# A decoder block on one Trainium2 core: rows of an expert table fetched without pacing, gate weights spread by one float32 matmul a token, and all 72 expert blocks ahead multiplied in whole float32

## The chip, the cores and the metric

One core of a Trainium2 chip runs one program. The metric is the device time of one execution in microseconds (us). Before the change the median of three runs is 1886.55 us (1883.9 to 1891.71). All rows below come from one profiled execution of 1878.31 us, whose span from the first to the last instruction is 1876.5 us.

## The reference, cut to what matters

512 tokens of width 1024 pass two token mixers and then an expert mixer (PEER) of 16384 experts; each token uses 128 of them (8 heads, 16 each). `u` and `v` have one row of 1024 for each expert.

```python
h = rms_norm(x, norm1_g)
proj = h @ w_in                                   # 1024 x 6400
y_a = hgrn2_mixer(...); y_b = dilated_attention_mixer(...)
merged = sigmoid(ga) * (y_a @ w_branch_a) + sigmoid(gb) * (y_b @ w_branch_b)
x = x + merged @ w_out
x = x + peer_ffn(rms_norm(x, norm2_g), w_q, sub_keys, u, v)

def peer_ffn(x, w_q, sub_keys, u, v):
    ...                                           # top 16 of two key sets, then top 16 of their sums: idx, gate
    hid = einsum('thkd,td->thk', u[idx], x)
    a = gelu(hid) * gate
    return einsum('thk,thkd->td', a, v[idx])
```

## The kernel before, in words

The 512 tokens are four tiles of 128 (0 to 3). They go through these stages, with their times in the profiled execution:

- **Front of tile 0** (to about 190 us): projections, both mixers, output projection, query projection.
- **Front of tiles 1 to 3** (190 to 705 us): the same for three tiles at once (`Front`, with `split`: each weight block `w` is loaded from HBM by SP (512 KB, two buffers), ScalarE rounds it to `wh`, VectorE or GpSimd forms the rest `wl` (`halves`, L98 and L99), and TensorE multiplies three products of halves (`accumulate`, L112)). First `mixers`: the projections of the HGRN2 mixer, its chunks, those of the attention, the attention, the gates. Then `post`: the branch products (L479), the output projection (`W_OUT`, added to x at L494), the norm (L500, L512), transposes, the query projection (`W_Q`).
- Beside it tile 0 is routed (`routing`: its experts and gates) and the **rows of u** of tile 0 are worked through: 128 steps, in each of which GpSimd issues an indirect DMA (`row`, L648) that fetches for each of the 128 tokens one row of u (128 x 1024 float32, 512 KB) and VectorE multiplies it with the token's vector and sums (L660). A row's buffer is one of three `rq` and one `row`, used in turn. `background`, called at each load of a weight block, asks for 1.8 such steps (`ROWS_F`) and sets `behind` to that load: by a manual dependency the row's DMA then waits until the weight load has landed. What is left of the 128 steps stands in `post` just ahead of the norm (`before_h2`).
- **The blocks ahead** (705 to 1065 us): `hidden(b)` for the first 72 (`NPRE`) of 128 blocks of experts: a block of `u` (tile `ub`, 512 KB) is multiplied with the 256 tokens of tiles 1 and 2, and GELU is taken. Blocks whose number divides by 3 (24 of 72) go as halves in three float32r products (tiles `uh`, `ul`), the others whole in float32 (tile `h32`, shown as `h`). Between them stand `routing` of tiles 3, 1 and 2, rows of u of tile 3, and the **scatter** (`scatter_steps`).
- **The scatter** writes for the tiles 1, 2 and 0 a dense table of weights, 128 x 128 experts for each token. It goes by groups of 4 tokens (96 groups in all; 4 groups to a `Gx` tile, which then goes to `g_d` in HBM). VectorE compares the two halves of the expert numbers with a ramp (`e12`, L697, bfloat16), multiplies the second with the three bfloat16 parts of the weight (`eg`, L701; in 88 groups the third part is done by ScalarE, four instructions, L705), TensorE does three bfloat16 matmuls a token (L711), ScalarE copies the sum out of PSUM (L713). Whatever of it is left after block 71 is drained (`scat(P)`), 1065 to 1126 us here.
- **The dense v stage** (1126 to 1845 us): 128 blocks of v, with the other 56 blocks of u as halves among them; rows of u and v of tile 3 beside it.

The order on each engine is made by a scheduler that works in the order of the program with a model of its own; each engine then runs its queue strictly in that order.

Of the kernel before, what the change touches and what calls it, by code (L numbers as in the profile page):

```python
# [18 lines left out]
P = 128  # L19
# [29 lines left out]

ROWS_F = 1.8  # L50

NPRE, RING = 72, 56

SPLIT = 3

ROUTE1, ROUTE2, SCAT_H = 12, 30, 2

GS, EGB = 4, 2
ACT3 = {0: (0, 4, 8, 12), 1: (0, 4, 8, 12), 2: (0, 4, 8)}

# [13 lines left out]
def kernel(ctx: ExitStack, tc: tile.TileContext, x, wst, par, cst, cols, g2, keys, u, v, ut, vr, out):  # L74
# [72 lines left out]
    class Front:  # L147
# [320 lines left out]

        def post(self, before_h2=lambda: None):

# [35 lines left out]
            h2s = hp.tile([P, NM // P, D], F32, name="pairA")  # L506
            before_h2()
            for t, T in enumerate(self.tiles):
# [36 lines left out]
    def route_bank(T):  # L545
        bank[0] += 1
        pt = pvg.tile([P, 512], F32, name="vg") if T and bank[0] % 2 else pr.tile([P, 512], F32, name="pr")
        return pt.rearrange("p (n k) -> p n k", k=NKEY)

    def thirds(i, x):  # L550

        w, dst = pk3[:, i], pk[:, i, 2:]
        nc.vector.tensor_copy(dst[:, 0], x)
        nc.vector.tensor_tensor(out=w, in0=x, in1=dst[:, 0], op=ALU.subtract)
        nc.vector.tensor_copy(dst[:, 1], w)
        nc.vector.tensor_tensor(out=w, in0=w, in1=dst[:, 1], op=ALU.subtract)
        nc.vector.tensor_copy(dst[:, 2], w)

    def routing(T, rq):
# [66 lines left out]
        if T in VD:  # L626
            pt = route_bank(T)
            i12 = rt.tile([P, 4, NKEY], F32, name="ssb")

            nc.vector.tensor_scalar(i12[:, 0], full, 1.0 / NKEY, -63.5 / NKEY, op0=ALU.mult, op1=ALU.add)  # L630
            nc.vector.tensor_scalar(i12[:, 0], i12[:, 0], RND, RND, op0=ALU.add, op1=ALU.subtract)
            nc.vector.scalar_tensor_tensor(i12[:, 1], i12[:, 0], -float(NKEY), full, op0=ALU.mult, op1=ALU.add)
            for j in range(2):
                nc.tensor.transpose(pt[:, 1 + j], i12[:, j], ident)
            nc.vector.tensor_copy(pk[:, VD.index(T), 0:2], pt[:, 1:3])
            if T in UD:
                nc.tensor.transpose(pt[:, 3], gate, ident)
                thirds(VD.index(T), pt[:, 3])

# [16 lines left out]
    def u_steps(T):  # L656
        g = UG.index(T)
        for j in range(P):
            r = row(idx[:, g, j:j + 1], u)
            nc.vector.scalar_tensor_tensor(r, r, 1.0, h2g[T], op0=ALU.mult, op1=ALU.mult,  # L660
                                           accum_out=hid[:, g, j:j + 1])
            yield 1
        with tc.high_priority():
            nc.scalar.activation(hid[:, g], hid[:, g], AF.Gelu)
            nc.vector.tensor_mul(hid[:, g], hid[:, g], gates[:, T])
            if T in VD:
                pt = pvg.tile([P, 512], F32, name="vg")
                nc.tensor.transpose(pt[:, :P], hid[:, g], ident)
                thirds(VD.index(T), pt[:, :P])

# [19 lines left out]
    def scatter_steps(T, bank):  # L690
        for i in range(0, P, GT):
            gi = VD.index(T) * (P // GT) + i // GT
            Gx = gb.tile([P, NKEY, GT], F32, name="Gx", bufs=2)
            for k in range(0, GT, GS):
                e = pk[:, VD.index(T), :, None, i + k:i + k + GS]
                e12 = gb.tile([P, 2, NKEY, GS], BF16, name="e12", bufs=2)
                nc.vector.tensor_tensor(out=e12, in0=iota[:, None].to_broadcast([P, 2, NKEY, GS]),  # L697
                                        in1=e[:, 0:2].to_broadcast([P, 2, NKEY, GS]), op=ALU.is_equal)
                eg = gb.tile([P, 3, NKEY, GS], BF16, name="eg", bufs=EGB)
                n = 2 if k in ACT3[T] else 3  # L700
                nc.vector.tensor_tensor(out=eg[:, :n], in0=e12[:, 1:2].to_broadcast([P, n, NKEY, GS]),  # L701
                                        in1=e[:, 2:2 + n].to_broadcast([P, n, NKEY, GS]), op=ALU.mult)
                if n == 2:
                    for q in range(GS):
                        nc.scalar.activation(eg[:, 2, :, q], e12[:, 1, :, q], AF.Copy,  # L705
                                             scale=pk3[:, VD.index(T), i + k + q:i + k + q + 1])
                for q0 in range(0, GS, 4):
                    pt = bank().rearrange("p (n k) -> p n k", k=NKEY)
                    for q in range(4):
                        for j in range(3):  # L710
                            nc.tensor.matmul(pt[:, q], e12[:, 0, :, q0 + q], eg[:, j, :, q0 + q],  # L711
                                             start=(j == 0), stop=(j == 2))
                    nc.scalar.activation(Gx[:, :, k + q0:k + q0 + 4].rearrange("p i t -> p t i"), pt, AF.Copy)  # L713
# [62 lines left out]

    pk = gat.tile([P, len(VD), 5, P], BF16, name="pk", bufs=1)
    pk3 = gat.tile([P, len(VD), P], F32, name="pk3", bufs=1)
    rctx = ctx.enter_context(ExitStack())
# [4 lines left out]
    def background(load):  # L784
        behind[:] = [load]
        rows(min(ROWS_F, P - rows.done))

# [3 lines left out]
    mixers(f)  # L791
    rq1, rq2, rq3 = f.post(lambda: rows(2 * P))
    hH, hL = f.hu
# [11 lines left out]
    def hidden(b, pool):  # L805
# [10 lines left out]
        pt = pool.tile([P, NU], F32, name="ph")  # L816
        if b < NPRE and b % SPLIT:
            accumulate(pt, [ub[:, k] for k in range(KC)], h32, slice(None), True)
# [123 lines left out]
```

## Time and profile before

| | |
|---|---|
| median of 3 runs | 1886.55 us |
| the profiled execution, and its span | 1878.31 us, 1876.5 us |
| TensorE busy | 1684.9 us, 90% of the span |
| VectorE busy | 1373.0 us, 73% |
| ScalarE busy | 784.2 us, 42% |
| GpSimd busy | 637.7 us, 34% |
| mean granted TensorE clock | 0.937 of 2.4 GHz |

Busy time of a matmul includes the drain of its pipeline, so that successive matmuls overlap; how long one really holds the engine is read from the starts of successive ones. One float32 matmul is two records in the trace, one of float32r or bfloat16 is one. "Idle before" in brackets behind a row is the time its engine had nothing running ahead of it, with what ended it.

### The profile page before, as it was taken

What the parts mean: (1) busy time and instruction counts of PE and PEld (TensorE: products, weight loads), DVE (VectorE), ACT (ScalarE), POOL (GpSimd) and SP (SyncE); (2) the same over time, 40 slices, a digit from 0 to 9 for tenths busy, and PEclk for the clock granted to TensorE, in tenths of its full rate; (3) what the DMA queues carried; (4) which work ended last, traced back from release to release, by engine and by line L of the source; (5) the groups of instructions that cost most, each with busy time, mean ns of one, the idle gap of its engine ahead of it and who ended that gap; (6) DMA issues with size and microseconds to landing.
All of it is one profiled execution on the core that took longest, in us unless ns stands there. A gap on an engine that the chain in (4) does not pass through costs nothing.

```text
span 1876.5 us, 28078 instructions
## 1 busy us (share of the span) xinstructions
PE 1684.9 (90%) x10301; PEld 1496.5 (80%) x10301; DVE 1373.0 (73%) x2793; ACT 784.2 (42%) x1466; POOL 637.7 (34%) x502
## 2 busy tenths in 40 slices
PE   8998889788986599999999889999999999989995
PEld 7887888687775489988899778888888888877774
DVE  2114999956567748988899777787778877777874
ACT  3324443333342436662366793343334333323331
POOL 0000455732323301434444104433434334444431
PEclk9999989889997789999999869999999999999998
DMA  8776478766567724755666539999999988888885
GB/s 277 249 234 206 137 249 292 226 230 197 174 213 241 280 79 146 276 208 201 213 223 208 208 127 346 325 343 325 337 321 337 343 314 309 311 287 309 311 301 179
DMA packets 173386, 473.49 MB, mean 252 GB/s; under 512 B 14784, under 2 KB 62144, under 8 KB 173248
## 3 DMA queue, kind: packets, MB, share of 16 engines
q1 hardware_dynamic: 115840, 268.47, 41.9%
q0 software_dynamic: 55296, 201.35, 30.5%
q10 hardware_dynamic: 2112, 1.88, 0.3%
q8 instruction: 81, 1.33, 0.3%
q14 instruction: 57, 0.47, 0.1%
HBM read 442.80 MB, written 27.79 MB: 251 GB/s over the span
## 4 chain that ended last, share of the span: by engine, by line
PE 51%; DMA 24%; DVE 14%; issue 5%; ACT 3%; POOL 2%; DVEq 0%; ACTq 0%; POOLq 0%; SPq 0%
PE acc L873 19%; PE ph L112 15%; PE pp L112 10%; DMA Gc<-g_d 7%; DMA w<-in_wst_dram 6%; PE pg L711 5%; DMA rq<-in_u_dram,idx 4%; DMA row<-in_u_dram,idx 2%; DVE rq L660 2%; DVE wl L99 2%; DMA rowx<-in_u_dram,idx 2%; DMA rowx<-in_v_dram,idx 1%; DVE Gc L862 1%; ACT eg L705 1%; DVE row L660 1%
## 5 line engine op out<-in xcount | busy, mean ns | idle before, releaser
L873 PE MATMUL acc<-vl,ah 128*128 128x512 f32 x768 | 242.3, 395 | 8.2 <-DVE vl L869 8.1
L873 PE MATMUL acc<-vh,al 128*128 128x512 f32 x768 | 241.4, 392 | 0.0
L873 PE MATMUL acc<-vh,ah 128*128 128x512 f32 x768 | 224.7, 398 | 10.8 <-ACT vh L867 10.8
L648 POOL DMA_INDIRECT rowx<-in_u_dram,idx x96 | 125.0, 1302 | 221.0 <-ACT pre L822 61.6
L648 POOL DMA_INDIRECT rowx<-in_v_dram,idx x96 | 133.0, 1385 | 189.2 <-DVE h2g L679 90.8
L112 PE MATMUL ph<-hH,ul 128*128 128x256 f32 x640 | 183.5, 287 | 8.2 <-DVE ul L99 8.2
L112 PE MATMUL ph<-hH,uh 128*128 128x256 f32 x640 | 187.2, 293 | 3.6 <-ACT pre L822 3.6
L112 PE MATMUL ph<-hL,uh 128*128 128x256 f32 x640 | 183.1, 286 | 0.0
L112 PE MATMUL ph<-h,ub 128*128 128x256 f32 x768 | 178.3, 387 | 4.2 <-DMA ub<-in_ut_dram 4.1
L660 DVE SCALAR_TENSOR_TENSOR rq<-rq,h2g 128x1024 f32<-128x1024 f32 x96 | 128.1, 1338 | 66.6 <-DMA rq<-in_u_dram,idx 66.5
L873 PEld LDWEIGHTS acc<-vl,ah 128*128 128x128 f32 x768 | 144.3, 190 | 40.2 <-DVE vl L869 11.7
L98 ACT ACTIVATE ah<-Gc 128x384 fp32r<-128x384 f32 x128 | 67.0, 524 | 261.1 <-PE acc L873 255.9
L873 PEld LDWEIGHTS acc<-vh,ah 128*128 128x128 f32 x768 | 144.3, 191 | 39.6 <-ACT vh L867 12.2
L648 POOL DMA_INDIRECT rq<-in_u_dram,idx x96 | 108.6, 1132 | 196.9 <-DMA w<-in_wst_dram 71.0
L873 PEld LDWEIGHTS acc<-vh,al 128*128 128x128 f32 x768 | 145.0, 189 | 30.0
L98 ACT ACTIVATE uh<-ub 128x1024 fp32r<-128x1024 f32 x80 | 85.1, 1064 | 193.4 <-PE ph L112 154.8
L112 PEld LDWEIGHTS ph<-h,ub 128*128 128x128 f32 x768 | 146.1, 195 | 24.0 <-issue 4.7
L869 DVE TENSOR_TENSOR vl<-vb,vh 128x1024 fp32r<-128x1024 f32 x128 | 156.3, 1221 | 8.3 <-ACT vh L867 8.2
L711 PE MATMUL pg<-eg,e 128*128 128x128 bf16 x1152 | 147.1, 297 | 13.3 <-ACT eg L705 7.1
L867 ACT ACTIVATE vh<-vb 128x1024 fp32r<-128x1024 f32 x128 | 135.8, 1061 | 35.7 <-DMA vb<-in_vr_dram 34.7
L711 PEld LDWEIGHTS <-e 128*128 128x128 bf16 x1152 | 129.3, 119 | 25.4 <-DVE eg L701 9.8
L98 ACT ACTIVATE wh<-w 128x512 fp32r<-128x512 f32 x144 | 88.5, 628 | 141.8 <-PE pp L112 79.9
(292 smaller groups left out, 3949.5 us busy)
## 6 DMA issues: line engine op xcount, KB each, us to landing
ub<-in_ut_dram SPq DMA_DIRECT2D x128, 512.0 KB, 5.2
vb<-in_vr_dram SPq DMA_DIRECT2D x128, 512.0 KB, 7.0
w<-in_wst_dram SPq DMA_DIRECT2D x107, 512.0 KB, 4.9
g_d<-Gx SPq DMA_DIRECT2D x24, 960.0 KB, 4.3
Gc<-g_d SPq DMA_DIRECT2D x15, 1536.0 KB, 16.3
wh<-in_wst_dram SPq DMA_DIRECT2D x37, 256.0 KB, 5.2
wl<-in_wst_dram SPq DMA_DIRECT2D x33, 256.0 KB, 4.8
pairB<-in_x_dram SPq DMA_DIRECT2D x5, 512.0 KB, 5.3
```

The source lines that it names most:

```text
L98: nc.scalar.activation(hi, x, AF.Copy)
L99: (eng or nc.vector).tensor_tensor(out=lo, in0=x, in1=hi.bitcast(F32), op=ALU.subtract)
L112: nc.tensor.matmul(out, l, r, start=(k == 0 and i == 0), stop=(k == last and i == len(ops) - 1))
L648: d = nc.gpsimd.indirect_dma_start(out=r, out_offset=None, in_=src, in_offset=bass.IndirectOffsetOnAxis(ap=index, axis=0))
L660: nc.vector.scalar_tensor_tensor(r, r, 1.0, h2g[T], op0=ALU.mult, op1=ALU.mult, accum_out=hid[:, g, j:j + 1])
L705: nc.scalar.activation(eg[:, 2, :, q], e12[:, 1, :, q], AF.Copy, scale=pk3[:, VD.index(T), i + k + q:i + k + q + 1])
L711: nc.tensor.matmul(pt[:, q], e12[:, 0, :, q0 + q], eg[:, j, :, q0 + q], start=(j == 0), stop=(j == 2))
L862: nc.vector.tensor_mul(gsl[:, :ngu], a.rearrange("p (g t) -> p g t", t=GT), gsl[:, :ngu])
L867: behind[:] = [nc.scalar.activation(vH, vb, AF.Copy)]
L869: nc.vector.tensor_tensor(out=vL, in0=vb, in1=vH.bitcast(F32), op=ALU.subtract)
L873: nc.tensor.matmul(acc[t][c], l.rearrange("p g t -> p (g t)")[:, t * P:(t + 1) * P], r[:, c * 512:(c + 1) * 512], start=(b == 0 and i == 0 ...
```

## The change

Three things. The rows of u in the front of tiles 1 to 3 no longer wait for a weight load (`behind` is not set there), 2.8 steps instead of 1.8 are asked for at each load, and the rest is asked for ahead of `post` instead of within it. The scatter makes `e1` (first half of the numbers) and `eg` (second half times the whole weight) in float32 and does one float32 matmul a token; the weight is kept whole (`pkw`) instead of in three parts (`thirds` goes); of the four groups to a `Gx` two have `eg` done by ScalarE (`ACTW`) and two by VectorE. All 72 blocks ahead are multiplied in whole float32.

```diff
-ROWS_F = 1.8
+ROWS_F = 2.8
-SPLIT = 3
-GS, EGB = 4, 2
-ACT3 = {0: (0, 4, 8, 12), 1: (0, 4, 8, 12), 2: (0, 4, 8)}
+GS = 4
+ACTW = (4, 12)
...
-            before_h2()
...
-                thirds(VD.index(T), pt[:, 3])
+                nc.vector.tensor_copy(pkw[:, VD.index(T)], pt[:, 3])
...
-                e = pk[:, VD.index(T), :, None, i + k:i + k + GS]
-                e12 = gb.tile([P, 2, NKEY, GS], BF16, name="e12", bufs=2)
-                nc.vector.tensor_tensor(out=e12, in0=iota[:, None].to_broadcast([P, 2, NKEY, GS]),
-                                        in1=e[:, 0:2].to_broadcast([P, 2, NKEY, GS]), op=ALU.is_equal)
-                eg = gb.tile([P, 3, NKEY, GS], BF16, name="eg", bufs=EGB)
-                n = 2 if k in ACT3[T] else 3
-                nc.vector.tensor_tensor(out=eg[:, :n], in0=e12[:, 1:2].to_broadcast([P, n, NKEY, GS]),
-                                        in1=e[:, 2:2 + n].to_broadcast([P, n, NKEY, GS]), op=ALU.mult)
-                if n == 2:
+                ti, tk = VD.index(T), slice(i + k, i + k + GS)
+                by_token = [P, GS, NKEY]
+                e1 = gb.tile(by_token, F32, name="e1", bufs=2)
+                nc.vector.tensor_tensor(out=e1, in0=iota[:, None, :, 0].to_broadcast(by_token),
+                                        in1=pk[:, ti, 0, tk, None].to_broadcast(by_token), op=ALU.is_equal)
+                e2 = gb.tile([P, NKEY, GS], BF16, name="e2", bufs=2)
+                nc.vector.tensor_tensor(out=e2, in0=iota, in1=pk[:, ti, 1, None, tk].to_broadcast([P, NKEY, GS]), op=ALU.is_equal)
+                eg = gb.tile(by_token, F32, name="eg", bufs=2)
+                if k in ACTW:
                     for q in range(GS):
-                        nc.scalar.activation(eg[:, 2, :, q], e12[:, 1, :, q], AF.Copy,
-                                             scale=pk3[:, VD.index(T), i + k + q:i + k + q + 1])
+                        nc.scalar.activation(eg[:, q], e2[:, :, q], AF.Copy, scale=pkw[:, ti, i + k + q:i + k + q + 1])
+                else:
+                    nc.vector.tensor_tensor(out=eg, in0=e2.rearrange("p k q -> p q k"),
+                                            in1=pkw[:, ti, tk, None].to_broadcast(by_token), op=ALU.mult)
...
-                        for j in range(3):
-                            nc.tensor.matmul(pt[:, q], e12[:, 0, :, q0 + q], eg[:, j, :, q0 + q],
-                                             start=(j == 0), stop=(j == 2))
+                        nc.tensor.matmul(pt[:, q], e1[:, q0 + q], eg[:, q0 + q], start=True, stop=True)
...
     def background(load):
-        behind[:] = [load]
         rows(min(ROWS_F, P - rows.done))
...
-    rq1, rq2, rq3 = f.post(lambda: rows(2 * P))
+    rows(2 * P)
+    rq1, rq2, rq3 = f.post()
...
-        if b < NPRE and b % SPLIT:
+        if b < NPRE:
             accumulate(pt, [ub[:, k] for k in range(KC)], h32, slice(None), True)
```

The change also moves instructions. Line numbers after the change are smaller by 2 to 12.

First VectorE's queue in the output projection of tiles 1 to 3, before (`wl` is the rest of a weight half, L494 adds a product to x, `rq`/`row` with h2g is a row of u):

```order
L494 TENSOR_TENSOR pairB<-pp,pairB 128x2x256
L99 TENSOR_TENSOR wl<-w,wh 128x512
L660 SCALAR_TENSOR_TENSOR rq,hid<-rq,h2g 128x1024
L660 SCALAR_TENSOR_TENSOR row,hid<-row,h2g 128x1024
L494 TENSOR_TENSOR pairB<-pp,pairB 128x256
L99 TENSOR_TENSOR wl<-w,wh 128x512 x2
L660 SCALAR_TENSOR_TENSOR rq,hid<-rq,h2g 128x1024
L99 TENSOR_TENSOR wl<-w,wh 128x512
L494 TENSOR_TENSOR pairB<-pp,pairB 128x2x256
L99 TENSOR_TENSOR wl<-w,wh 128x512
L660 SCALAR_TENSOR_TENSOR rq,hid<-rq,h2g 128x1024 x2
L660 SCALAR_TENSOR_TENSOR row,hid<-row,h2g 128x1024
```

and after, the same place:

```order
L492 TENSOR_TENSOR pairB<-pp,pairB 128x2x256
L97 TENSOR_TENSOR wl<-w,wh 128x512
L492 TENSOR_TENSOR pairB<-pp,pairB 128x256
L97 TENSOR_TENSOR wl<-w,wh 128x512 x3
L492 TENSOR_TENSOR pairB<-pp,pairB 128x2x256
```

The rows of u have left this place. Counted over VectorE's queue: up to the 48th `wl` of this front 53 rows stand ahead in both; up to the 84th 94 before and 109 after; up to the 90th (the last branch products) 99 before and 125 after; after that 29 before and 3 after. Between the sum of squares (L500) and the norm of the last tile (L512) six rows stood; after the change there stand four comparisons and a product of the scatter (`e1`, `e2`, `eg`) and two more `e2` behind them.

Second, SP's queue at the end of the blocks ahead, before (`ub` loads a block of u, `g_d<-Gx` stores four finished groups of the scatter, `vb` is the first load of the dense v stage):

```order
L815 DMA ub<-in_ut_dram 128x1024 x4
L715 DMA g_d<-Gx 128x1920
L815 DMA ub<-in_ut_dram 128x1024
L715 DMA g_d<-Gx 128x1920
L815 DMA ub<-in_ut_dram 128x1024
L715 DMA g_d<-Gx 128x1920 x8
L865 DMA vb<-in_vr_dram 128x1024 x3
```

and after:

```order
L804 DMA ub<-in_ut_dram 128x1024 x4
L704 DMA g_d<-Gx 128x1920
L804 DMA ub<-in_ut_dram 128x1024
L704 DMA g_d<-Gx 128x1920
L804 DMA ub<-in_ut_dram 128x1024
L704 DMA g_d<-Gx 128x1920 x2
L855 DMA vb<-in_vr_dram 128x1024 x3
```

Eight stores behind the last block before, two after. On TensorE's queue 408 scatter matmuls (34 groups at 12) stand behind the last matmul of the blocks before, 40 (10 groups at 4) after; in both the block 72, in halves, already stands ahead of them.

Third, VectorE's queue in the later part of the scatter, two groups before (`e_` and a number is e12 there):

```order
L697 TENSOR_TENSOR e_8368<-iota,pk 128x1024
L539 MATCH_REPLACE rest<-sv,cs 128x50
L697 TENSOR_TENSOR e_8390<-iota,pk 128x1024
L701 TENSOR_TENSOR eg<-e_8368,pk 128x1024
L540 MAX sv<-rest 128x8
L701 TENSOR_TENSOR eg<-e_8390,pk 128x1024
```

and two groups after (L687 makes e1, L690 e2):

```order
L687 TENSOR_TENSOR e_8399<-iota,pk 128x512
L696 TENSOR_TENSOR eg<-e_8401,pkw 128x512
L687 TENSOR_TENSOR e_8411<-iota,pk 128x512
L648 SCALAR_TENSOR_TENSOR rowx,hid<-rowx,h2g 128x1024
L690 TENSOR_TENSOR e_8463<-iota,pk 128x512
L690 TENSOR_TENSOR e_8475<-iota,pk 128x512
```

Four instructions of 1024 elements become five of 512, and `e2` stands a pair of groups ahead of its use.

## Rows read from the trace of the kernel before

**Rows 1.** The head of the page: span, and busy time, share and instructions of each engine.
```profile
span 1876.5 us, 28078 instructions
PE 1684.9 (90%) x10301; PEld 1496.5 (80%) x10301; DVE 1373.0 (73%) x2793; ACT 784.2 (42%) x1466; POOL 637.7 (34%) x502
```

**Rows 2.** Busy time of each engine by stage. Columns: stretch and length, then PE, PEld, DVE, ACT, POOL busy us (instructions), granted TensorE clock, DMA share, GB/s.
```profile
190.00:400.00 210.00, 174.91 (x1178) 164.14 (x1178) 193.03 (x470) 78.25 (x152) 119.02 (x90) 0.90 0.69 230
400.00:545.00 145.00, 129.25 (x973) 111.24 (x972) 85.91 (x178) 55.77 (x113) 39.56 (x38) 0.91 0.58 192
545.00:705.00 160.00, 115.52 (x681) 108.68 (x680) 103.68 (x183) 53.90 (x121) 38.80 (x34) 0.83 0.59 204
705.00:1065.00 360.00, 345.13 (x2191) 314.55 (x2189) 315.02 (x991) 206.29 (x427) 135.07 (x107) 0.98 0.61 212
1065.00:1126.00 61.00, 49.44 (x384) 42.99 (x384) 47.27 (x67) 60.16 (x129) 4.41 (x9) 0.66 0.34 139
1126.00:1845.00 719.00, 690.07 (x3580) 590.48 (x3581) 567.63 (x733) 264.15 (x365) 294.68 (x212) 0.98 0.91 320
```

**Rows 3.** The same for the rows of u alone (L660 on VectorE; each row is two instructions, the product and a short read of its sum).
```profile
400.00:545.00 145.00, 43.34 (x70) 0.91 0.58 192
545.00:705.00 160.00, 41.40 (x68) 0.83 0.59 204
```

**Rows 4.** VectorE's waits: what waited for what, us in total, times, longest. The first two are of 190 to 545 us, the third of 545 to 705 us.
```profile
DVE rq L660 <- DMA rq<-in_u_dram,idx: 47.4, 20, 5.1
DVE row L660 <- DMA row<-in_u_dram,idx: 14.4, 8, 3.7
...
DVE rq L660 <- DMA rq<-in_u_dram,idx: 19.1, 10, 5.1
```

**Rows 5.** The chain that ended last, in the output projection of tiles 1 to 3: start, us, what.
```profile
602.68 1.21 DVE wl L99 x2
...
603.90 3.94 DMA w<-in_wst_dram
...
608.63 4.45 DMA rq<-in_u_dram,idx
...
614.41 1.22 DVE wl L99 x2
615.64 5.85 DMA w<-in_wst_dram
```

**Rows 6.** The timeline from the output projection to the query projection: its first matmul, then on VectorE the sum of squares, a row of u, and the norm of the last tile; last, two pieces of the chain that ended last, the query projection's matmuls.
```profile
578.67 0.47 PE L112 MATMUL pp<-wh,hT 128*128 128x256 f32 x1 [3.37 <-DVE pairB L479]
...
639.64 0.17 DVE L500 TENSOR_REDUCE ssx<-ssx 128x3 f32<-128x12 f32 x1
642.75 1.22 DVE L660 SCALAR_TENSOR_TENSOR rq<-rq,h2g 128x1024 f32<-128x1024 f32 x1 [2.94 <-DMA rq<-in_u_dram,idx]
657.98 1.28 DVE L512 SCALAR_TENSOR_TENSOR h2g<-pairB,ssx,kT 128x1024 f32<-128x1024 f32 x1
...
663.53 20.81 PE pp L112 x108
693.72 6.12 PE pp L112 x34
```

**Rows 7.** TensorE's timeline in two places at a granted clock of 1.00: a whole block in halves (24 matmuls from the first row to the second), 28 records of whole float32 blocks, 24 scatter matmuls, and what follows; then two runs of eight records of float32 128 x 128 matmuls in the front of tile 0.
```profile
768.92 0.39 PE L112 MATMUL ph<-hH,uh 128*128 128x256 f32 x1
...
771.87 6.21 PE L112 MATMUL ph<-h,ub 128*128 128x256 f32 x28
777.91 3.00 PE L711 MATMUL pg<-eg,e 128*128 128x128 bf16 x24
780.73 1.04 PE L112 MATMUL ph<-h,ub 128*128 128x256 f32 x4
...
13.25 1.06 PE L112 MATMUL pp<-hT,wh 128*128 128x128 f32 x8
14.14 1.06 PE L112 MATMUL pp<-hT,wl 128*128 128x128 f32 x8
```

**Rows 8.** ScalarE's timeline in the drain of the scatter; no row there has idle time ahead of it.
```profile
1092.89 2.07 ACT L713 ACTIVATE Gx<-pg 128x512 f32<-128x512 f32 x2
1094.77 1.46 ACT L705 ACTIVATE eg<-e,pk 128x128 bf16<-128x128 bf16 x4
1095.97 1.16 ACT L713 ACTIVATE Gx<-pg 128x512 f32<-128x512 f32 x1
...
1100.27 2.07 ACT L713 ACTIVATE Gx<-pg 128x512 f32<-128x512 f32 x2
```

**Rows 9.** Groups of instructions by shape on VectorE: out<-in, shapes, count | busy us, mean ns of one | idle before.
```profile
L697 DVE TENSOR_TENSOR e<-iota,pk 128x1024 bf16<-128x1024 bf16 x96 | 72.6, 764 | 27.6 <-PE pg L711 27.6
L701 DVE TENSOR_TENSOR eg<-e,pk 128x1536 bf16<-128x1536 bf16 x8 | 7.7, 958 | 0.3
L99 DVE TENSOR_TENSOR wl<-w,wh 128x512 fp32r<-128x512 f32 x124 | 89.4, 732 | 31.0 <-ACT wh L98 29.8 <-issue 1.2
L99 DVE TENSOR_TENSOR ul<-ub,uh 128x1024 fp32r<-128x1024 f32 x80 | 104.9, 1311 | 24.2 <-ACT uh L98 23.8
```

**Rows 10.** DMA issues with KB and median us from issue to landing, and the group of GpSimd's row DMAs with what its queue waited for.
```profile
w<-in_wst_dram SPq DMA_DIRECT2D x107, 512.0 KB, 4.9
rq<-in_u_dram,idx POOLq DMA_INDIRECT x96, 5.8
...
L648 POOL DMA_INDIRECT rq<-in_u_dram,idx x96 | 108.6, 1132 | 196.9 <-DMA w<-in_wst_dram 71.0
```

More of the change, by code (lines that the diff above doesn't have):

```diff
@@ L467, in proj_gates, with post @@
                         nc.scalar.activation(dst[:, 2 * b:2 * b + 2], dst[:, 2 * b:2 * b + 2], AF.Sigmoid)
-        def post(self, before_h2=lambda: None):
+        def post(self):
             ga, gb, N, n = self.ga, self.gb, self.N, self.n
@@ L548, in route_bank @@
         return pt.rearrange("p (n k) -> p n k", k=NKEY)
[L550 to L557, printed above, removed]
     def routing(T, rq):
@@ L668, in u_steps @@
                 nc.tensor.transpose(pt[:, :P], hid[:, g], ident)
-                thirds(VD.index(T), pt[:, :P])
+                nc.vector.tensor_copy(pkw[:, VD.index(T)], pt[:, :P])
     def v_steps(T):
@@ L775 @@
     hid = gat.tile([P, len(UG), P], F32, name="hid", bufs=1)
-    pk = gat.tile([P, len(VD), 5, P], BF16, name="pk", bufs=1)
-    pk3 = gat.tile([P, len(VD), P], F32, name="pk3", bufs=1)
+    pk = gat.tile([P, len(VD), 2, P], BF16, name="pk", bufs=1)
+    pkw = gat.tile([P, len(VD), P], F32, name="pkw", bufs=1)
     rctx = ctx.enter_context(ExitStack())
```

## The prediction

> **What bounds the kernel now.** The page's head comes first [rows 1]: TensorE is busy 90% of the span, so it is the first suspect, but the share is a mean over unlike stages. The windows by stage [rows 2] take it apart. In 705 to 1065 us (the blocks ahead, the "loop") TensorE is busy 345 of 360 us at a clock of 0.98, while VectorE has 315: TensorE sets the end, VectorE stands close behind. In 1065 to 1126 us (the "tail", where the rest of the scatter is drained) ScalarE is busy 60.2 of 61 us and TensorE at a clock of 0.66: ScalarE sets the end. In 545 to 705 us no engine is full (115 and 104 of 160) and the clock is at 0.83: waits set the end. The dense v stage is TensorE's (690 of 719) and the change leaves it alone.
>
> Which waits, the chain of waits says [rows 5]: in the output projection a round goes from a weight's rest `wl` (602.68) to the next weight load, from that to the DMA of a row of u, which waits for it, to VectorE, which waits for the row ahead of the next `wl` (614.41): 11.7 us a round, each step behind the last. VectorE's waits show the same over a longer stretch: 47.4 + 14.4 = 61.8 us for rows in 190 to 545 us, 19.1 in 545 to 705 [rows 4]. GpSimd's row DMAs stood 71.0 us behind `w` loads [rows 10].
>
> **The scatter on TensorE.** 24 scatter matmuls in bfloat16 take 777.91 to 780.73 [rows 7], 0.1175 us each: a group of 4 tokens (12 matmuls) 1.41 us. Of float32 128 x 128 matmuls, two records each, 8 records take 13.25 to 14.14: 0.111 a record, 0.222 a matmul, 0.89 a group. The 96 groups lose 96 x 0.52 = 50 us. As these rows come from another stage, the bounds are 0.222 and, if each float32 matmul cost four times the bfloat16 row, 0.47 a token; I take 0.222, a measured matmul of the same shape.
>
> The Trainium skill, "FP8 and Floating Point Precision", section "TensorE Precision Notes", says that true float32 takes four passes through the array; "TensorE: Matmul & The Clock Gate", "Back-to-back issue gap", gives 134 cycles for 128 columns. By these pages alone a token would go from three passes to four, an estimate of +56 ns x 384 = +21 us instead of -50, and the sum would end 71 us later. The float32 row agrees (0.222 is four such gaps); the bfloat16 row doesn't: 0.1175 us, twice the gap. So the trace has three of the old matmuls dearer than one of the new.
>
> **The 24 blocks, whole.** A block in halves takes 768.92 to 771.87 = 2.95 us; 28 records of whole float32 blocks take 771.87 to 777.91, 0.2157 each, a block (16 records) 3.45 [rows 7]. TensorE gets +0.50 x 24 = +12 us. ScalarE loses 24 `uh`, VectorE 24 `ul`, 1.31 us each in the group by shapes [rows 9], some 1.22 each back to back as two `wl` halves are (1.21 for two [rows 5]): -29 us.
>
> **The loop together.** Before: 48 x 3.45 + 25 x 2.95 + 62 x 1.41 = 327 us of these on TensorE (62 of the 96 groups stand ahead of its last block by the order, and 25 blocks in halves, block 72 among them). After: 72 x 3.45 + 2.95 + 86 x 0.89 = 328. The loop stays at some 361 us, but 86 groups stand in it instead of 62. That fits only if VectorE keeps up. A pair of groups costs it 4 x 0.60 = 2.4 us before (the 1024-element bfloat16 instructions average 764 ns, with overlap; 0.60 is the 512-element float32 `wl` spacing, 1.21 for two, which I take for both). After: two `e1` 1.20, one `eg` 0.60, and two `e2` in bfloat16, bounded by 0.33 (half of 0.60 and a little, from 764 at 1024 and 958 at 1536 elements [rows 9]) and 0.60; at 0.33 the pair is 2.46. So 24 more groups add 12 x 2.46 = 30 us, the `ul` take 29 out, and the rest is even: VectorE 315 + some 7 = 322 of 361. If `e2` takes 0.60, 86 groups add 23 us and VectorE stands at 345, still under. ScalarE has 206 of 360 and loses work.
>
> **The tail.** 34 groups remain behind the last block before, 10 after (the order of TensorE's queue). Of four groups ScalarE does four copies from PSUM and three products of four instructions: 1092.89 to 1100.27 = 7.38 us with no idle time [rows 8], the products 1.20 each (1094.77 to 1095.97), so the copies (7.38 - 3.60)/4 = 0.95. After, only two of four groups have products there: 4 x 0.95 + 2 x 1.20 = 6.2 us, 1.55 a group, 10 groups 16 us. The tail goes from 61 to 16 us, -45; one more activation table load and a loop 1 us longer leave **-43**. The bounds: with VectorE the limit instead of ScalarE (2.46 a pair) the same 10 groups take 12 us; with 24 groups slipping back into the tail at 1.55, 53 us.
>
> `thirds`, five short instructions, becomes one copy: nothing, beside the routing's 20-odd us. Two more half blocks stand ahead of the first matmul of the v stage, 2.6 us that move from one side of a border to the other.
>
> **The rows of u in the front.** Three places.
> (a) The output projection runs 578.67 to 639.64 = 61 us [rows 6] for 8 weight loads. The query projection, the same count of loads without rows, takes 663.53 to 699.84 (693.72 + 6.12) = 36 us, 4.5 a load. By the order no row is left in the output projection after the change. With some 10 us for its start (the drain of the gates) it should take 46: **-15**; bounds 0 and -25.
> (b) Between the sum of squares (639.64) and the query projection (663.53) lie 23.9 us, in which VectorE works off 6 rows at 1.22 and waits 2.94 for one: 10 us out. Four comparisons and a product of the scatter come in, some 3 us: **-7**.
> (c) The mixers. By the order, up to the last branch products 125 rows stand ahead on VectorE instead of 99: 26 more x 1.3 (43.34 us over 35 rows with their short reads is 1.24 [rows 3]) = +34 us of work, against 61.8 us of waits for rows, which unpaced rows should mostly not meet: four buffers hold rows that were asked for long before. VectorE is busy 193 of 210 us in 190 to 400 but 86 of 145 in 400 to 545 [rows 2]: crowded first, free later. Bounds +34 and -28 (34 - 62); I take **-5**, as the waits stood partly beside TensorE's work (129 of 145 busy).
> Front: -27.
>
> **The sum.** The profiled execution is 1878.3 us; 1878.3 - 43 - 27 = 1808. The median of the runs stands 8.2 us above it, so as a median **1816 us**, -3.7%. About 0.5% (9 us) is what a measurement here tells from no change.
>
> **The rivals**, as medians.
> *Forecast*: tail and front both give; 0.59, own range 1790 to 1838.
> *The front gives nothing*: VectorE's in-order queue holds the 26 rows ahead of what the mixers' matmuls wait for, and post's gain is paid back there. For it: 193 of 210. Against: 59 us idle in 400 to 545. 1886.5 - 43 = 1843; 0.18.
> *VectorE becomes the loop's bound*: 322 (or 345) of 361 in a strictly ordered queue, with routing and rows of tile 3 between; comparisons come late, matmuls of the scatter hold TensorE, and only about 10 of the 43 remain: 1886.5 - 10 - 27 = 1849; 0.12. With the one before together, 1876, within 0.5% or just past it: 0.03.
> *Slower: rows crowd out the weight loads.* A weight lands in 4.9 us, a row in 5.8 [rows 10]. Unpaced, up to four rows of 512 KB stand in the queues beside a load. The busiest stage moves 320 GB/s [rows 2], at which a row takes 1.6 us; a load behind four of them lands in 4.9 + 6.5 = 11.4 us. Two `w` buffers at 4.5 us a load hide 9.0; the excess of 2.4 x some 50 loads = 120 us. With the tail's -43 and half of the front's: 1886.5 - 65 + 120, about 1940. It decides from a landing of 10.3 us on (1.3 x 50 = 65). Against it: the DMA engines are busy 0.58 to 0.69 in the front at 190 to 230 GB/s, so there is room, and VectorE's own pace (1.24 a row, but in order between other work) holds the rows to one in some 3 us. 0.05.
> *Slower: a float32 matmul at 0.47 us a token*: 384 x (0.47 - 0.3525) = +45 instead of -50; 1816 + 95 = 1911. Against it stand both runs of eight records [rows 7]. 0.03.
>
> **How the numbers follow.** The likeliest is 1816. The range of eight in ten goes from 1778 (mixers at their -28 and `e2` at its low bound: 1816 - 23 - 15) to 1860 (front or VectorE holding, with room for a few us more). Faster by over 0.5%: 0.59 + 0.18 + 0.12 less the edge of the last, 0.88; same 0.04; slower 0.08.
>
> **What the profile after would show.** Tail: some 16 us between the last block ahead and the first of v, 10 groups at about 1.55; the scatter's TensorE records 768 at 0.111 each; if these show 0.2, the price is wrong. Loop: some 361 us with TensorE over 340 busy; if VectorE is above 345 with TensorE waiting for `e1` or `eg`, the third case is there. Output projection: no row of u, some 46 us; the gap to the query projection some 17. Mixers: waits of VectorE for rows below 30 us in 190 to 545, and TensorE not waiting longer for VectorE's `wl`. Weight loads still landing in about 5 us; 8 or more with TensorE waiting for them is the fourth case. Wrong would be the forecast above all if the mixers grow by more than post loses, or if groups beyond 10 run behind the last block in time although they stand ahead of it in the queue.

## The result, and the profile after

The changed kernel takes 1809.24 us (median of 4 runs, 1805.38 to 1812.82) against 1886.47 us (4 runs) before: ratio 0.9587, 95% interval 0.9555 to 0.9618, 77 us less. The profiled executions differ by 73.0 us in span (1876.5 and 1803.5). The forecast was 1816 us. The total came out as forecast, but two of its parts did not: the front gave twice what was put down, and loop, tail and end together gave 19 us instead of 43. That the two misses cancel is luck.

The head of the page, and from its list of DMA issues the weight loads (KB, median us to landing). They answer to [rows 1, 10]:

```profile
span 1803.5 us, 26810 instructions
PE 1639.0 (91%) x9725; PEld 1450.2 (80%) x9725; DVE 1346.3 (75%) x2805; ACT 700.8 (39%) x1283; POOL 641.5 (36%) x502
...
w<-in_wst_dram SPq DMA_DIRECT2D x107, 512.0 KB, 5.2
```

The windows by stage, first of the kernel before, cut at the events that the changed kernel has too (the stages of [rows 2] have other borders), then of the changed kernel. Columns as in [rows 2]. The stages: mixers of tiles 1 to 3; output projection; sum of squares to first query matmul; query projection, to the first scatter matmul; blocks ahead to the last of them (the loop); the rest of the scatter (the tail); dense v stage and end.

```profile
190.00:578.60 388.60, 328.69 (x2274) 298.17 (x2273) 303.47 (x691) 142.86 (x279) 173.39 (x142) 0.91 0.66 219
578.60:639.60 61.00, 42.82 (x288) 40.47 (x288) 44.22 (x72) 19.59 (x45) 20.17 (x18) 0.81 0.73 246
639.60:661.20 21.60, 5.70 (x25) 4.93 (x26) 17.92 (x29) 6.95 (x12) 3.82 (x3) 0.50 0.57 220
661.20:700.90 39.70, 38.38 (x211) 36.76 (x210) 13.45 (x24) 15.87 (x46) 0.00 (x0) 0.92 0.27 93
700.90:1061.30 360.40, 346.20 (x2199) 315.60 (x2198) 315.99 (x1003) 205.25 (x423) 135.07 (x107) 0.98 0.61 211
1061.30:1126.80 65.50, 52.47 (x410) 45.66 (x408) 50.66 (x73) 64.25 (x139) 4.41 (x9) 0.67 0.34 139
1126.80:1876.50 749.70, 700.27 (x3624) 598.59 (x3624) 574.62 (x740) 265.28 (x366) 294.68 (x212) 0.97 0.89 312
```

```profile
190.00:557.50 367.50, 319.37 (x2268) 289.74 (x2266) 335.12 (x738) 144.20 (x282) 210.59 (x162) 0.92 0.77 264
557.50:598.60 41.10, 35.94 (x288) 34.87 (x288) 21.35 (x34) 19.31 (x44) 0.00 (x0) 0.99 0.46 156
598.60:611.00 12.40, 5.64 (x24) 4.70 (x24) 11.41 (x19) 6.06 (x14) 0.00 (x0) 0.50 0.34 127
611.00:647.30 36.30, 36.30 (x209) 34.94 (x208) 12.31 (x16) 13.47 (x39) 0.00 (x0) 0.99 0.30 102
647.30:1025.90 378.60, 356.91 (x1951) 317.78 (x1950) 318.69 (x1056) 171.69 (x349) 133.52 (x113) 0.96 0.63 212
1025.90:1049.70 23.80, 12.86 (x81) 11.78 (x80) 16.98 (x32) 16.73 (x33) 1.60 (x3) 0.86 0.52 207
1049.70:1803.50 753.80, 701.12 (x3624) 599.22 (x3624) 576.38 (x740) 265.26 (x366) 289.57 (x212) 0.97 0.88 311
```

Stage by stage: mixers -21.1, output projection -19.9, norm -9.2, query projection -3.4 (front: -53.6); loop **+18.2**, tail -41.7, the rest +4.1; together -73.0. In the loop after, TensorE is busy 357 of 379 us at a clock of 0.96; before 346 of 360 at 0.98.

VectorE's waits for rows in 190 to 545 us (us in total, times, longest), and what GpSimd's row DMAs waited for in the same stretch, first after, then before:

```profile
DVE rq L648 <- DMA rq<-in_u_dram,idx: 19.6, 19, 2.8
DVE row L648 <- DMA row<-in_u_dram,idx: 7.1, 7, 1.4
...
POOL rq L636 <- DVE rq L648: 52.9, 39, 4.7
```

```profile
POOL rq L648 <- DMA w<-in_wst_dram: 42.8, 7, 8.4
POOL rq L648 <- DVE rq L660: 26.0, 15, 4.7
...
POOL row L648 <- DMA w<-in_wst_dram: 14.7, 4, 6.6
```

The 61.8 us of [rows 4] are 26.7. GpSimd stood behind weight loads for 57.5 us; after the change it stands behind VectorE, which gives the buffers back (52.9 us on `rq` instead of 26.0): VectorE's own pace sets the rows.

TensorE's timeline at a clock of 1.00: two groups of the scatter (16 records, 8 matmuls) and the whole float32 blocks behind them:

```profile
769.25 1.95 PE L701 MATMUL pg<-eg,e 128*128 128x128 f32 x16
771.04 8.37 PE L110 MATMUL ph<-h,ub 128*128 128x256 f32 x38
```

1.79 us for 16 records is 0.112 each, 0.224 a token. The price of [rows 7] holds.

What TensorE waited for in the loop, and VectorE:

```profile
PE pg L701 <- DVE eg L696: 10.3, 5, 3.5
PE pg L701 <- DVE e L687: 4.7, 4, 3.3
```

```profile
DVE rowx L648 <- DMA rowx<-in_u_dram,idx: 23.3, 10, 4.9
...
DVE row L648 <- DMA row<-in_u_dram,idx: 10.2, 3, 4.9
```

The same waits in the loop before:

```profile
DVE rowx L660 <- DMA rowx<-in_u_dram,idx: 12.0, 10, 2.6
...
DVE row L660 <- DMA row<-in_u_dram,idx: 2.8, 4, 1.6
...
PE pg L711 <- DVE eg L701: 2.6, 2, 1.8
```

VectorE waited 33.5 us for rows (23.3 + 10.2) instead of 14.8 (12.0 + 2.8), TensorE 10.3 for `eg` instead of 2.6. And in slices of 50 us, the loop after the change (same columns):

```profile
647.30:700.00 52.70, 49.42 (x280) 44.12 (x280) 51.41 (x209) 26.94 (x55) 17.93 (x16) 0.97 0.51 179
700.00:750.00 50.00, 45.42 (x253) 39.53 (x251) 47.94 (x156) 23.56 (x47) 18.05 (x17) 0.93 0.60 205
750.00:800.00 50.00, 46.72 (x228) 41.08 (x228) 48.83 (x227) 16.11 (x33) 21.60 (x18) 0.93 0.63 210
800.00:850.00 50.00, 46.63 (x235) 40.49 (x234) 38.79 (x124) 14.01 (x31) 19.67 (x15) 0.97 0.59 195
850.00:900.00 50.00, 44.74 (x246) 40.02 (x245) 49.42 (x175) 22.47 (x48) 20.78 (x17) 0.97 0.61 206
900.00:950.00 50.00, 48.08 (x266) 43.01 (x265) 42.08 (x98) 27.13 (x55) 19.77 (x16) 0.97 0.68 229
950.00:1000.00 50.00, 50.00 (x294) 45.71 (x293) 27.30 (x51) 25.73 (x54) 11.19 (x11) 1.00 0.77 263
```

In 647 to 800 us VectorE is busy 148 of 153 us and TensorE lacks 11; in 950 to 1000 it is 27 of 50 and TensorE is full. The mean of 319 of 379 hides both.

### The profile page after: what moved, and what is told of

It reads as the page before. It is cut to its first block, busy times and chain, and to the rows that moved or that the text cites. A ratio compares the mean times of both kernels' runs of the same rounds, so it can differ in the third digit from the quotient of the medians.

```text
span 1803.5 us, 26810 instructions
## 1 busy us (share of the span) xinstructions
PE 1639.0 (91%) x9725; PEld 1450.2 (80%) x9725; DVE 1346.3 (75%) x2805; ACT 700.8 (39%) x1283; POOL 641.5 (36%) x502
## 4 chain that ended last, share of the span: by engine, by line
PE 47%; DVE 25%; DMA 21%; issue 4%; ACT 2%; POOL 1%; DVEq 0%; POOLq 0%; ACTq 0%; SPq 0%
PE acc L863 18%; PE pp L110 16%; DMA Gc<-g_d 9%; PE ph L110 9%; DMA w<-in_wst_dram 2%; DMA rq<-in_u_dram,idx 2%; DVE e L687 2%; DVE rowx L648 2%; PE pg L701 2%; DMA rowx<-in_u_dram,idx 2%; DVE rq L648 1%; DVE row L648 1%; DVE eg L696 1%; DMA row<-in_u_dram,idx 1%; DVE wl L97 1%
## 5 line engine op out<-in xcount | busy, mean ns | idle before, releaser
L110 PE MATMUL ph<-h,ub 128*128 128x256 f32 x1152 | 265.4, 386 | 0.0
L110 PEld LDWEIGHTS ph<-h,ub 128*128 128x128 f32 x1152 | 219.2, 195 | 29.8 <-issue 0.2
L636 POOL DMA_INDIRECT rq<-in_u_dram,idx x96 | 120.0, 1250 | 93.5 <-DVE rq L648 52.9
L648 DVE SCALAR_TENSOR_TENSOR rowx<-rowx,h2g 128x1024 f32<-128x1024 f32 x96 | 122.4, 1276 | 39.2 <-DMA rowx<-in_u_dram,idx 39.1
L648 DVE SCALAR_TENSOR_TENSOR rq<-rq,h2g 128x1024 f32<-128x1024 f32 x96 | 132.8, 1385 | 19.8 <-DMA rq<-in_u_dram,idx 19.6
L110 PE MATMUL ph<-hH,ul 128*128 128x256 f32 x448 | 127.6, 285 | 5.1 <-DVE ul L97 5.1
L110 PE MATMUL ph<-hH,uh 128*128 128x256 f32 x448 | 127.8, 285 | 3.8 <-ACT pre L812 3.8
L667 DVE SCALAR_TENSOR_TENSOR h2g<-rowx,hid,h2g 128x1024 f32<-128x1024 f32 x95 | 121.7, 1281 | 8.4 <-DMA rowx<-in_v_dram,idx 8.0
L110 PE MATMUL ph<-hL,uh 128*128 128x256 f32 x448 | 127.7, 285 | 0.0
L701 PE MATMUL pg<-eg,e 128*128 128x128 f32 x768 | 104.5, 290 | 23.5 <-DVE eg L696 17.3
```

Of the source, the lines that this page charges most:

```text
L110: nc.tensor.matmul(out, l, r, start=(k == 0 and i == 0), stop=(k == last and i == len(ops) - 1))
L636: d = nc.gpsimd.indirect_dma_start(out=r, out_offset=None, in_=src, in_offset=bass.IndirectOffsetOnAxis(ap=index, axis=0))
L667: nc.vector.scalar_tensor_tensor(acc, r, hid[:, g, j:j + 1], acc, op0=ALU.mult, op1=ALU.add)
L701: nc.tensor.matmul(pt[:, q], e1[:, q0 + q], eg[:, q0 + q], start=True, stop=True)
```

## The experiments

Two questions were left: which edit shortened the front, above all the mixers, and what lengthened the loop. Besides the ratio, one length is compared, "blocks and tail": from the first scatter matmul to the first matmul of the v stage, each in the one profiled execution (433.5 us before, 412.0 after).

**Each part alone.** The rows' edits on the kernel before:

```diff
-ROWS_F = 1.8
+ROWS_F = 2.8
-        behind[:] = [load]
-    rq1, rq2, rq3 = f.post(lambda: rows(2 * P))
+    rows(2 * P)
+    rq1, rq2, rq3 = f.post()
```

> The kernel before with the change of the rows of u alone: no wait for a weight load in the front of tiles 1 to 3, 2.8 steps a load, the rest ahead of the output projection. Theory A (the two traces: the front of tiles 1 to 3 shrank by 53.5 us, from a first scatter matmul at 700.9 to one at 647.3, and the scatter has no part in it): 53 us less, ratio about 0.972; first scatter matmul at 645 to 650. Theory B (VectorE's lighter scatter and the lighter blocks behind the front helped it, or rows that no longer fit in the loop cost there): 27 us less or fewer, as forecast for the front, ratio 0.985.

Measured: 0.9749 (0.9705 to 0.9793), 48 us less; first scatter matmul at 650.7 instead of 700.9. Theory A: the front's whole gain is the rows'. Blocks and tail 434.3, as before.

The scatter alone (the scatter's part of the diff, `b % 3` kept for the blocks, rows as before):

> The kernel before with the float32 scatter alone; a third of the blocks ahead stay halves, the rows are as before. Order: 28 groups behind the last block ahead instead of 34. Theory A (TensorE sets the loop, ScalarE the tail): loop 48 x 3.45 + 25 x 2.95 + 68 x 0.89 = 300 instead of 327, so 27 us less if VectorE allows it, tail 28 x 1.55 = 43 instead of 61, together 45 us less, ratio 0.976. Theory B (VectorE's in-order queue, with rows of u that wait for their DMA ahead of comparisons, sets the loop once TensorE is lighter): loop no shorter than now, only the tail's 18 us, ratio 0.990.

Measured: 0.9815 (0.9777 to 0.9854), 35 us less, between the two. Blocks and tail 412.9 us, already as short as in the changed kernel (412.0). Its loop, and what TensorE waited for in it:

```profile
698.30:1057.10 358.80, 325.87 (x1999) 296.33 (x1998) 325.93 (x1037) 168.56 (x323) 138.63 (x109) 0.97 0.61 215
...
PE pg L702 <- DVE eg L697: 17.3, 9, 4.9
```

TensorE is busy 20 us less than before (346 to 326), and the loop is as long as before (358.8 to 360.4), with VectorE busy 326 of it: once TensorE is lighter, the loop does not follow, as theory B had it; VectorE's queue, which TensorE waits for, is the likeliest end. Of the 28 us less in the profiled execution 18 are the tail's, 65.5 to 47.2.

The whole blocks alone:

```diff
-        if b < NPRE and b % SPLIT:
+        if b < NPRE:
```

> The kernel before with all 72 blocks ahead in whole float32 and nothing else; scatter in bfloat16, rows as before. Order: 24 groups behind the last block ahead instead of 34. Theory A (TensorE sets the loop): 72 x 3.45 + 2.95 + 72 x 1.41 = 353 instead of 327, +26 us in the loop, tail 24 x 1.845 = 44 instead of 61, -17: +9 us, ratio 1.005. Theory B (VectorE and ScalarE, relieved of 24 ul and uh, let the loop run better): 15 us less, ratio 0.992.

Measured: 1.0031 (1.0007 to 1.0055), 7 us more: theory A.

```profile
703.80:1084.60 380.80, 372.93 (x2127) 330.75 (x2126) 305.82 (x1000) 205.21 (x444) 125.55 (x110) 0.99 0.59 206
```

TensorE is busy 373 us (+27) of a loop that is 20 us longer; the tail gives 18 back.

Rows and scatter without the whole blocks (the changed kernel with `b % 3` again):

> The changed kernel, but a third of the blocks ahead in halves as before: rows of u and scatter are those of the change. Theory A (parts add up, whole blocks cost TensorE 12 us and gain little): like the changed kernel or better, 1790 to 1805 us, ratio 0.950 to 0.957. Theory B (whole blocks are what lets VectorE place 24 more groups in the loop: 28 groups stand behind the last block here, 10 in the changed kernel): 15 to 25 us slower than the changed kernel, ratio 0.968 or so.

Measured: 0.9632 (0.9593 to 0.967), 1818 us, against 0.9587 (0.9555 to 0.9618) of the changed kernel. That lies between the two theories. The changed kernel, with whole blocks, is 9 us lower, but these intervals overlap, the two were not timed side by side, and blocks and tail differ by 3 us only (415.0 against 412.0): a gain of the whole blocks is not shown. Nor do the parts add up: rows alone gave 48 us and the scatter alone 35, the two together 67 and not 83; where the 16 us go stays open.

**The front: wait, rate or place.** The changed kernel with the wait put back:

```diff
+        behind[:] = [load]
         rows(min(ROWS_F, P - rows.done))
```

> The changed kernel with the wait of each row's DMA for a weight load put back in the front of tiles 1 to 3 (behind is set again), 2.8 steps a load and the rest ahead of the output projection as in the changed kernel; VectorE's queue has the rows at the same places as in the changed kernel, so the wait alone differs. Theory A (the wait costs the mixers; the place of the rows gives the output projection's and the norm's gain): the first output projection matmul at 575 to 590 instead of 557.6, the output projection still 41 to 46 us long and the norm chain 12 us, ratio 0.966 to 0.975. Theory B (the place of the rows gives all): as the changed kernel, ratio 0.956 to 0.962.

Measured: 0.9607 (0.958 to 0.9635), as the changed kernel; first output projection matmul at 564.6, VectorE's waits for rows 25.6 us in 190 to 545. Theory A falls: the wait costs nothing here.

No wait, but 1.8 steps and the rest in the output projection's part as before:

> The changed kernel with 1.8 steps a load and the rest asked for in the output projection's part, as before, but without the wait for a weight load. By the order VectorE's queue has the rows where the changed kernel has them (109 ahead of the 84th wl, 125 ahead of the 90th). Theory A (the wait is the whole of the front's change; the number of steps and the place in the program do nothing without it): within 0.5% of the changed kernel, ratio 0.954 to 0.963. Theory B (steps asked for early keep the four buffers full): 10 us or more slower, ratio over 0.964.

Measured: 0.9614 (0.9564 to 0.9665), as the changed kernel: theory A. Once the wait is gone, rate and place do nothing that these runs can tell.

One number changed in the kernel before:

```diff
-ROWS_F = 1.8
+ROWS_F = 2.8
```

> The kernel before with one number changed: 2.8 steps of the rows of u at each weight load instead of 1.8; the wait for that load and the place of the rest stay. By the order VectorE's queue then has the rows where the changed kernel has them (109 ahead of the 84th wl instead of 94, 125 ahead of the 90th instead of 99). Theory A (the rate is what counts: at 2.8 a row waits for a load that landed long ago, and all 128 are asked for by the 46th load): as the rows' change alone, ratio 0.971 to 0.979, output projection 41 to 43 us. Theory B (the wait costs by itself): 0.980 or more.

Measured: 0.9725 (0.9667 to 0.9784): all of the rows' gain, with the wait in place: theory A. Output projection from 559.1, query projection from 613.5.

The changed kernel with the wait and 1.8 steps:

> The changed kernel with the wait for a weight load put back and 1.8 steps a load, so that of the rows' change only the place of the rest (ahead of the output projection) is left. By the order 104 rows stand ahead of the 90th wl (99 before, 125 in the changed kernel), the last 24 in the output projection, none at the norm. Theory A (rate and wait together set the rows' pace; the place alone only frees the norm chain): first output projection matmul at 575 to 583, output projection 52 to 62 us, norm chain 12 us; 25 to 40 us slower than the changed kernel, ratio 0.972 to 0.981. Theory B (the place of the rest is what counts): within 8 us of the changed kernel, ratio 0.957 to 0.965.

Measured: 0.9764 (0.9707 to 0.9822), 28 us slower than the changed kernel. The mixers end at 585.3 (a little later than theory A's 575 to 583), the output projection takes 55.6 us, the norm chain 13.1: theory A. GpSimd's waits in 190 to 545 of this kernel, and its row in the kernel with the one number changed:

```profile
POOL rq L636 <- DMA w<-in_wst_dram: 39.3, 6, 8.5
...
POOL row L636 <- DMA w<-in_wst_dram: 18.7, 4, 8.0
```

```profile
POOL rq L648 <- DVE rq L660: 62.2, 44, 4.7
```

So it was wait and rate together. At 1.8 steps each row waits for the load that it was asked with, and 128 rows would need 71 loads (128 / 1.8); at 2.8 they need 46, and the buffers, given back by VectorE, are what the DMA waits for, with the wait or without it. Either edit alone gives the same.

**The loop: VectorE's load or its rows.** All four `eg` on ScalarE:

```diff
-ACTW = (4, 12)
+ACTW = (0, 4, 8, 12)
```

> The changed kernel with the product eg of all four groups of a Gx on ScalarE (two of four before). VectorE loses 48 x 0.6 = 29 us, ScalarE gains 48 x 1.2 = 58, most of it in a loop in which it is busy 172 of 379 us. Order: 2 groups behind the last block ahead instead of 10. Theory A (VectorE's in-order queue makes the 15 us that TensorE waits in the loop for eg and e1, and the 8 us in the tail): loop and tail together 380 to 388 us instead of 402, ratio 0.949 to 0.952. Theory B (VectorE's waits for rows of u, 33 us in the loop, hold comparisons up whatever VectorE's load; or ScalarE's own queue holds eg behind a GELU that waits for TensorE): no gain, ratio 0.957 to 0.963.

Measured: 0.9677 (0.9623 to 0.9732): no gain, theory B. VectorE is busy 300 us in the 382 from 643 to 1025 and TensorE still waits (12.7 us for `e1`); VectorE waits 36.6 us there for rows. Blocks and tail 405.1, 7 us shorter, as at their end the hand-over to the v stage stands behind a row in VectorE's queue:

```profile
1047.06 1.22 DVE L648 SCALAR_TENSOR_TENSOR rowx<-rowx,h2g 128x1024 f32<-128x1024 f32 x1 [5.87 <-DMA rowx<-in_u_dram,idx]
...
1048.21 2.77 DVE L852 TENSOR_TENSOR Gc<-pre,Gc 128x256 f32<-128x256 f32 x8
```

Why the whole is not 7 us shorter but longer stays open: from the first to the last matmul of its v stage 733 us passed in the profiled execution; the same stage took 715 to 732 in the other kernels with rows in the loop.

The same with a third of the blocks in halves:

> As the run with all eg on ScalarE, and a third of the blocks ahead in halves as before the change: VectorE has 24 ul (29 us) more, ScalarE 24 uh (25 us) more, TensorE 12 us less. Order: 10 groups behind the last block. Theory A (with VectorE relieved, halves pay again, as TensorE's 48 x 3.5 + 25 x 2.95 + 86 x 0.97 = 325 and some 20 of routing set the loop at 350 to 360; tail 10 x 2.15 = 22): loop and tail 372 to 382, ratio 0.944 to 0.949. Theory B (VectorE, again at 318 of busy time, keeps the loop at 378): ratio 0.957 to 0.961.

Measured: 0.9586 (0.9553 to 0.9618), as the changed kernel; blocks and tail 408.7. Theory B. It is also 19 us faster than the run before it, timed beside it (1796 to 1807 us against 1809 to 1827), although its blocks and tail are 4 us longer: from the first v matmul to the end its profiled execution takes 734 us against 754. Why, no run shows.

No rows of u among the blocks ahead:

```diff
-ROWS_H, ROWS_D = 0.6, 1.9
+ROWS_H, ROWS_D = 0.0, 2.1
```

> The changed kernel without rows of u among the blocks ahead (0 instead of 0.6 steps a block); tile 3's rows are all worked through in the dense v stage, 2.1 steps a block there instead of 1.9. Order: 2 groups behind the last block ahead instead of 10. Theory A (rows that VectorE waits for, 33 us in the loop, stand ahead of comparisons in its queue and make TensorE wait): TensorE waits under 8 us for e1 and eg, loop and tail together 370 to 382 us instead of 402. Theory B (VectorE's rows have nothing to do with it; TensorE's 357 us and the routing's waits set the loop): 392 or more. The dense v stage takes 43 rows (54 us of VectorE) more, of 567 in 727 busy: 0 to 35 us longer; ratio 0.945 to 0.965.

Measured: loop and tail 370.7 us instead of 402.4, as theory A has it (TensorE still waits 10.4 us for `eg`, more than the 8 of the expectation). The run takes out the rows' work on VectorE (57 us in the loop) together with their waits, and does not tell the two apart. But the whole is 0.9927 (0.9901 to 0.9953), not 0.945 to 0.965. Loop and tail of this kernel, its v stage and end, and one of the last rows of v:

```profile
655.60:1026.30 370.70, 356.35 (x2024) 318.46 (x2024) 279.06 (x996) 185.28 (x378) 80.99 (x71) 0.99 0.47 165
1036.00:1873.00 837.00, 696.58 (x3602) 594.24 (x3601) 624.74 (x820) 263.30 (x363) 344.59 (x256) 0.92 0.86 305
...
1840.37 1.28 DVE L667 SCALAR_TENSOR_TENSOR h2g<-row,hid,h2g 128x1024 f32<-128x1024 f32 x1
```

TensorE's v matmuls end at 1765.5, 20 us ahead of the changed kernel's (1785.1), and then VectorE works off rows of v of tile 3 until 1842: 2.1 steps a block were not reached in that stage. The expectation priced the 43 rows as VectorE time (54 us in 160 idle) and did not ask at what pace the stage takes rows; what holds them there was not tried. By GpSimd's waits it is the buffers: its row DMAs stood 241 us behind VectorE's work on earlier rows (176 in the changed kernel), and 29 behind the `vh` that they are made to wait for.

The same with a third of the blocks in halves:

> The same with a third of the blocks ahead in halves as before the change: TensorE 12 us less, VectorE 29 us and ScalarE 25 us more in the loop. Order: 4 groups behind the last block. Theory A (with the rows out VectorE has room for the 24 ul, some 294 of 350, and halves pay again): loop and tail 358 to 370 us, 10 us or more shorter than with whole blocks and no rows. Theory B (halves make TensorE wait for ul and eg as much as they save): within 5 us of that run or longer.

Measured: loop and tail 366.5, 4 us shorter than with whole blocks, theory B, though blocks and tail are 374.1 against 380.6; the whole 0.9894 (0.983 to 0.9958), again held by the rows at the end. With the rows out of the way halves come out 11 us lower in the median and 6.5 lower in blocks and tail; the intervals overlap.

## Why the prediction was right, step by step

- **Price of the scatter on TensorE.** Right: 0.224 us a token (forecast 0.222, was 0.3525). The rival of 0.47 is out. The Trainium skill, "FP8 and Floating Point Precision", section "TensorE Precision Notes", gives true float32 four passes; with the isolated gap of 134 cycles for 128 columns in "TensorE: Matmul & The Clock Gate", section "Back-to-back issue gap", that is an estimate of 0.223 us, and the trace agrees. With that section's some 81 ns for a stream with weight loads it would be an estimate of 0.324, and there the trace does not. By the isolated gap three bfloat16 passes would have been cheaper (0.168); there [rows 7] disagree with 0.3525, and the measurement decides.
- **Tail.** Right: 10 groups from 1030.6 to 1047.2, 1.66 each (forecast 1.55). The stage lasted 23.8 instead of 16: 2.5 us are the wait behind the last group for ScalarE, and 4.7 come of a row of u in VectorE's queue at its head, whose DMA GpSimd had issued late:

```profile
1019.92 1.71 POOL L636 DMA_INDIRECT rowx<-in_u_dram,idx  x1 [9.74 <-ACT keys_sb L812]
...
1027.72 1.22 DVE L648 SCALAR_TENSOR_TENSOR rowx<-rowx,h2g 128x1024 f32<-128x1024 f32 x1 [4.67 <-DMA rowx<-in_u_dram,idx]
1028.87 0.08 DVE L648 DVE_READ_ACCUMULATOR rowx<-rowx,h2g 128x1 f32 x1
1028.87 0.42 DVE L690 TENSOR_TENSOR e<-iota,pk 128x512 bf16<-128x512 bf16 x1
1029.21 0.68 DVE L687 TENSOR_TENSOR e<-iota,pk 128x512 f32<-128x512 bf16 x1
1029.81 0.68 DVE L696 TENSOR_TENSOR eg<-e,pkw 128x512 f32<-128x512 bf16 x1
1030.41 0.68 DVE L687 TENSOR_TENSOR e<-iota,pk 128x512 f32<-128x512 bf16 x1
```

  VectorE's rows here confirm the prices on VectorE: 0.60 for `e1` and `eg`, 0.34 for `e2` (forecast 0.60, 0.60, 0.33).
- **The loop, "That fits only if VectorE keeps up".** This step failed: forecast 361 us, measured 378.6. VectorE's busy time was right (forecast 322, measured 319; the "some 7" in it had no working, and +30 and -29 would have given 316), the conclusion from it was not. A mean of 322 in 361 was read as room; but the routing fills VectorE in the first part (148 of 153 us), and its strictly ordered queue holds comparisons behind rows that wait for their DMA (33.5 us instead of 14.8). TensorE's idle time grew from 14.2 to 21.7 us. The other 10.7 us is busy time: 356.9 instead of 346.2, where the sum had +1, at a granted clock of 0.96 instead of 0.98. The run without rows in the loop shows both parts: the same matmuls (but for six), tail included, took TensorE 356 us at a clock of 0.99, and 370 (356.9 + 12.9) in the changed kernel. Without the rows among the blocks the loss is gone (370.7 for loop and tail, against 361 + 16 in the forecast); whether their waits or their work make it, no run tells apart. The waits have an origin that the prediction did not look at: the change leaves the wait of these rows for a block's GELU (`behind`) in place, and GpSimd's row DMAs stood 103 us behind GELUs in the loop (83 before), the one at the head of the tail 9.7. No run takes that wait out. The rival in which VectorE becomes the loop's bound described this place; it priced the loss at 33 us, and 20 came true (loop and tail gave 23.5 of the 43).
- **The mixers (c).** Direction right, size wrong: -5 taken, bounds -28 to +34, measured -21.1. Of this some 4 us belong to the single execution: in the ten executions with this VectorE order the first output projection matmul stood at 557.6 to 570.3, mean 563; in the three with the old one at 577.5 to 584.5, mean 580; so -17. The term was discounted "as the waits stood partly beside TensorE's work"; 35 us fewer waits of VectorE became 11.8 us less idle time of TensorE (59.9 to 48.1) and 9.3 less busy time (328.7 to 319.4) for the same work. The clock rose from 0.91 to 0.92 only, some 4 us by proportion; the rest of the 9.3 stays open.
- **The output projection (a)** took 41.1 us, not 46: the 10 us of start, which no row had shown, were not needed, and the clock was 0.99 instead of 0.81. **The norm chain (b)**: -9.2 against -7. The query projection, put at no change, gave 3.4 at a clock of 0.99 instead of 0.92.
- **What the row edit does.** The prediction spoke of rows freed from the wait. The runs show that the wait by itself cost nothing at 2.8 steps, and the rate nothing without the wait: the prediction named one half of the mechanism.
- **Rows against weight loads.** Direction right, size far from deciding: a load lands in 5.2 us (median of all; 6.1 instead of 4.9 in 190 to 545), not 10.3. In that stretch ScalarE waits 41.7 us for loads instead of 25.6, and TensorE 17.7 for `wl` instead of 15.5, where the forecast had no longer wait.
- **Whole blocks.** Where TensorE sets the loop they cost the +12 (+7 us alone, after what the tail gives back). With the light scatter the sign is not settled: whole blocks came out 9 us lower in the changed kernel (overlapping intervals, not timed side by side), 19 higher with all `eg` on ScalarE, 11 higher without rows in the loop. That this third edit gains anything is not shown.

So the total of -70 in the forecast's sum against -73.0 holds two errors: the front gave 27 us more than forecast, and loop, tail and end together 24 less. The forecast of the total was right by luck in this: the front's excess covered for the loop.

## What to carry to other kernels

An engine's mean busy time over a stage says whether work fits in it only if the stage is even: cut it into slices first, and look what else is queued ahead of the new work on an engine that runs strictly in order. A transfer that is made to wait for its turn need not lose time by the wait or by a slow rate alone, as here it took both; ask what it would wait for next if the first wait went. And when a long stage is short of one engine, moving its filler (rows, here) elsewhere only pays if the other stage can take it at its own pace.

## What the runs showed of the hardware

The clock is part of the price of a wait: the same float32 matmuls took TensorE 356 us where it had 14 us of gaps (clock 0.99) and 370 where it had 33 (0.96, and 0.86 in the tail). Busy time times clock is nearly the same in the two, 353 and 354, so within the rounding the clock accounts for the difference. And kernels whose VectorE queue is the same up to a point reached that point up to 13 us apart (557.6 to 570.3), which is more than the 0.4% by which the four runs of the changed kernel differ in the whole (1805 to 1813; another kernel's four went from 1801 to 1820); the length of a stage in a single execution is to be read with that in mind.
